# The first projection of a streaming encoder: program order on every engine, two token blocks in turn, a wide norm

## The chip, the cores and the metric

The kernel runs on one core of a Trainium2 chip. The metric is the time of one execution on the device in microseconds. Five engines of the core work side by side, each through its own queue: TensorE (PE, with its weight loads as PEld), VectorE (DVE), ScalarE (ACT), GpSimd (POOL) and SyncE (SP), which here only issues transfers. SBUF holds the working tiles and PSUM the sums of matmuls.

## The reference, cut to what matters

One layer of an encoder, for a prompt of 2048 tokens and a sample of 32, both with D = 1024 channels. The part that the change touches is the beginning:

```python
shift_m, scale_m, gate_m, shift_f, scale_f, gate_f = adaln_modulation(c, p['w_ada'], p['b_ada'])
h = rmsnorm(x, p['g_pre_mix']) * (1.0 + scale_m) + shift_m
z = h @ p['w_in']
qa, ka, va, qb, kb, vb, gb, gk_low, gate_a, gate_b = jnp.split(z, np.cumsum(IN_SIZES)[:-1].tolist(), axis=-1)
```

`adaln_modulation` is `silu(c) @ w_ada + b_ada`, split in six; `rmsnorm` divides a token by the root of its mean square and multiplies with a gain. Attention over a band of chunks, gated linear attention, two gated branches, an output projection and a feed-forward part with a short convolution follow; the change leaves them alone. The columns `qb` and `kb` of `w_in` (256 each) are the first that the kernel computes.

## The kernel before, in words

All tokens (2080, the sample last) stand with channels on the partitions: D is eight pieces of 128, named k. Every product is made in three passes, with operands split in a high part and a rest (`mm3`, lines 78 to 80: high by high, high by rest, rest by high). `hA[0]` and `hA[1]` keep the high part and the rest of `h` for the first 1664 tokens, `hB` for the last 416; `hB` takes the memory of the pool `ada`, once that is closed.

The first projection computes `h` and its products with 512 columns (two chunks of 128 for `Q`, two for `K`) for five blocks b of 416 tokens. The norm goes by half blocks of 208 (`NH`), numbered 0 to 9 (`hb` before, `u` after), since 2048 is inside the last one: there `parts` returns two pieces, 176 tokens of the prompt and 32 of the sample, with scale and shift of their own.

Steps of a half block before the change: `prep_load` (line 262) brings two tiles `xk` of four k each; six buffers. `prep_stats` squares two k at a time on ACT (lines 271 and 274) and adds them (275, 276), on DVE for half blocks 0 and 1, on GpSimd for the others. `rstd_bcast` splits the sum (`sh`, `sl`, lines 69 and 72), sums over partitions with a matmul by ones (148, 149), which also spreads the result, and finishes with Ln, Exp (154, 155) and one Newton step in three DVE operations (156 to 158); the part from the matmul on runs when the function that it returns is called. `prep_apply` then does, for each k, `x * scale * r` on DVE (294), the high part with the shift on ACT (295), and the rest on DVE (296). For half block 2, four k have the first step on GpSimd (`prep_scale`, and line 292).

The scale and shift come from `ada(j, v)`: v = 1 scale, v = 0 shift, j one of four pieces of 256 channels. `ada_load` brings two halves of 512 KB (`wa`, six buffers); 16 matmuls (line 315), a copy to SBUF (318), four matmuls that turn the result (322), and `mod_finish` on DVE (134, 138) into `mod`. So a k can only be shifted after the ada piece of its channels.

`wave(b, ks_, ps, chunks)` runs the matmuls of a block for some k, 12 per k with four chunks. `wave_evac` writes the sums out through `t_evac`: Q chunks are copied on ACT (line 225), K chunks on DVE (228), both to a tile `tx` that has two buffers, and stored to DRAM by a transfer that ACT issues (line 230). The weights of the two column groups come in four pieces each (`w_pieces`, lines 185 to 187: load to `wr`, high part on ACT, rest on DVE).

The order of TensorE's instructions is that of the program text throughout (a `manual_schedule` over PE). The other engines are ordered by the planner of the compiler by priority and its own costs, apart from later stages, which put all five engines in program order. Block 0's waves are laced with the ada pieces by hand; blocks 1 to 4 follow in a loop `s_`, where the half block two ahead is prepared. Behind the first projection, line 515 onwards, come six groups of columns with tokens on the partitions (`n_tile`, matmuls `pn`), beside which bias tables and the late modulation are made.

Of the kernel before, what the change touches and what calls it, by code (L numbers as in the profile page):

```python
# [10 lines left out]
F32 = mybir.dt.float32  # L11
# [9 lines left out]
KD = 8  # L21
# [37 lines left out]
def encoder_step(ctx: ExitStack, tc: tile.TileContext, I, O):  # L59
# [178 lines left out]
    with ExitStack() as st:  # L238
# [16 lines left out]
        XK = {}  # L255
        POOL = {2: (1, 3, 5, 7)}

        def prep_load(hb, q_=nc.sync):
            XK[hb] = []
            for k in range(0, KD, 4):  # L260
                x = pp.tile([128, 4, NH], F32, name="xk", tag="xk", bufs=6)
                q_.dma_start(x, dap(I["xT"], k * 128 * T + NH * hb, [[T, 128], [128 * T, 4], [1, NH]]))
                XK[hb].append(x)

        def prep_stats(hb, add):

            sq = pp.tile([128, 2, NH], F32, name="sq", tag="sq", bufs=2)
            for k in range(0, KD, 2):
                x = XK[hb][k // 4][:, k % 4:k % 4 + 2]
                if k == 0:  # L270
                    nc.scalar.activation(sq, x, AF.Square)
                    continue
                s2 = pp.tile([128, 2, NH], F32, name="sq2", tag="sq2")
                nc.scalar.activation(s2, x, AF.Square)
                add.tensor_add(sq, sq, s2)
            add.tensor_add(sq[:, 0], sq[:, 0], sq[:, 1])
            return lambda: rstd_bcast(pp, psx, "px", sq[:, 0], NH, NH, 2)

        def prep_scale(hb):
            for k in POOL.get(hb, ()):  # L280
                for a, e, s in parts(NH * hb, NH):
                    xs = XK[hb][k // 4][:, k % 4, a:e]
                    nc.gpsimd.tensor_scalar(xs, xs, mod[:, 1, k, s:s + 1], 1.0, op0=OP.mult, op1=OP.mult)

        def prep_apply(hb, r, ks_=range(KD)):
            for k in ks_:
                for a, e, s in parts(NH * hb, NH):
                    hi, lo = [h_at(x, k, NH * hb + a, e - a) for x in range(2)]
                    xs = XK[hb][k // 4][:, k % 4, a:e]
                    s1, s2 = mod[:, 1, k, s:s + 1], mod[:, 0, k, s:s + 1]  # L290
                    if k in POOL.get(hb, ()):
                        nc.gpsimd.tensor_mul(xs, xs, r[:, a:e])
                    else:
                        nc.vector.scalar_tensor_tensor(xs, xs, s1, r[:, a:e], op0=OP.mult, op1=OP.mult)
                    nc.scalar.activation(hi, xs, AF.Identity, bias=s2)
                    nc.vector.scalar_tensor_tensor(lo, xs, s2, f32(hi), op0=OP.add, op1=OP.subtract)
# [3 lines left out]
        def ada_load(j, v):  # L300

            PIECE[j, v] = []
            for half in range(2):
                w = pa.tile([128, 4, 256], F32, name="wa", tag="wa", bufs=6)
                nc.sync.dma_start(w, dap(I["w_ada"], half * 512 * 6 * D + v * D + 256 * j,
                                         [[6 * D, 128], [128 * 6 * D, 4], [1, 256]]))
                PIECE[j, v].append(w)

        def ada(j, v):


            p = psx.tile([128, 512], F32, name="pm", tag="px")
# [5 lines left out]
            nc.vector.tensor_copy(r, p[:, :256])  # L318
# [9 lines left out]
        ln_exp_table()  # L328
        ada_load(0, 1)
        prep_load(0)  # L330
        prep_load(1)
        ada_load(0, 0)
        first = [("Q", 1536), ("K", 1792)]
        w0, steps = zip(*[w_pieces(wp, c0, 256, 272, 2, 2) for _, c0 in first])

        def wave(b, ks_, ps, chunks=range(4)):
            for k in ks_:
                for i in chunks:
                    mm3(ps[i][:, :NB], [t_terms(w0[i // 2], 128 * (i % 2), b, k)], first=k == 0, last=k == KD - 1)

        def wave_tiles():
            return [psx.tile([128, 512], F32, name="px", tag="px") for _ in range(4)]

        def wave_evac(b, ps):
            for i in range(4):
                t_evac(stg, first[i // 2][0], i % 2, b, ps[i][:, :NB])

        fin0 = prep_stats(0, nc.vector)()
        ada_load(1, 1)
        for s_ in steps:  # L350
            s_[0]()
        ada_load(1, 0)
        m0 = ada(0, 1)
        r0 = fin0()
        fin1 = prep_stats(1, nc.vector)()
        m1 = ada(0, 0)
        m0()
        r1 = fin1()
        ps = wave_tiles()
        fins = {}  # L360
        for s_ in steps:
            s_[1]()
        ada_load(2, 1)
        prep_load(2)
        m0 = ada(1, 1)
        m1()
        m1 = ada(1, 0)
        m0()
        ada_load(2, 0)
        ada_load(3, 1)  # L370
        prep_load(3)
        prep_apply(0, r0, [0, 1])
        prep_apply(1, r1, [0, 1])
        for s_ in steps:
            s_[2]()
        ada_load(3, 0)
        fins[2] = prep_stats(2, nc.gpsimd)
        wave(0, (0, ), ps)
        m1()
        m0 = ada(2, 1)  # L380
        prep_apply(0, r0, [2, 3])
        prep_apply(1, r1, [2, 3])
        prep_load(4)
        for s_ in steps:
            s_[3]()
        wave(0, (1, ), ps)
        m0()
        m1 = ada(2, 0)
        fins[3] = prep_stats(3, nc.gpsimd)
        wave(0, (2, ), ps)  # L390
        m1()
        m0 = ada(3, 1)
        prep_apply(0, r0, [4, 5])
        prep_apply(1, r1, [4, 5])
        wave(0, (3, ), ps)
        m0()
        prep_scale(2)
        m1 = ada(3, 0)
        r2 = fins.pop(2)()()
        wave(0, (4, ), ps)  # L400
        m1()
        prep_apply(0, r0, [6, 7])
        prep_apply(1, r1, [6, 7])
        prep_apply(2, r2)
        prep_load(5)
        wave(0, (5, ), ps)
        f3 = fins.pop(3)()
        wave(0, (6, ), ps)
        r3 = f3()
        wave(0, (7, ), ps)  # L410
        prep_apply(3, r3)
        fins[4] = prep_stats(4, nc.gpsimd)
        wave_evac(0, ps)
# [3 lines left out]
        for s_ in range(2, 10):  # L417
            b = s_ // 2
            if s_ + 4 < 10:
                prep_load(s_ + 4)  # L420
            if s_ + 3 < 10:
                fins[s_ + 3] = prep_stats(s_ + 3, nc.gpsimd)
            k0 = 4 * (s_ % 2)
            if s_ + 2 < 10:
                fin = fins.pop(s_ + 2)()
            if s_ % 2 == 0:
                ps = wave_tiles()
            if b < 4:
                wave(b, range(k0, k0 + 1), ps)
                prep_apply(s_ + 2, fin())  # L430
                wave(b, range(k0 + 1, k0 + 4), ps)
            elif s_ % 2 == 0:

                wave(b, range(KD), ps, (0, 1))
                wn = load_w(wp, 2048, 256, 272, 2, 2)
            else:
                wave(b, range(KD), ps, (2, 3))
# [1893 lines left out]
```

## Time and profile before

| | |
|---|---|
| runs shown | 3172.7, 3176.35, 3173.73 us; median 3173.73 |
| the profiled execution, its own time | 3174.99 us |
| its span in the trace | 3173.3 us |
| granted TensorE clock, mean | 0.992 |
| PE, DVE, ACT, POOL busy | 3056.5, 2243.6, 1649.5, 263.7 us |
| first wave of the first projection | starts at 26.86 us |
| last wave of the first projection | ends at 159.66 us |

Times in the trace count from the start of the span. A row of a group of instructions gives line, engine, operation, tile written and tiles read, shapes, count, then busy time and the mean of one in ns, then the idle time ahead of them on that engine with what ended it. A row of the timeline begins with start and length. In a row of waits stand who waited, for whom, the total, how often, and the longest. Queues of transfers are marked with a q behind the engine that issues them.

### The profile page before, as it was taken

What the parts mean: (1) busy time and instruction counts of PE and PEld (TensorE: products, weight loads), DVE (VectorE), ACT (ScalarE), POOL (GpSimd) and SP (SyncE); (2) the same over time, 40 slices, a digit from 0 to 9 for tenths busy, and PEclk for the clock granted to TensorE, in tenths of its full rate; (3) what the DMA queues carried; (4) which work ended last, traced back from release to release, by engine and by line L of the source; (5) the groups of instructions that cost most, each with busy time, mean ns of one, the idle gap of its engine ahead of it and who ended that gap; (6) DMA issues with size and microseconds to landing.
All of it is one profiled execution on the core that took longest, in us unless ns stands there. A gap on an engine that the chain in (4) does not pass through costs nothing. (4 is left out here: it accounts for less than half of the span.)

```text
span 3173.3 us, 56451 instructions
## 1 busy us (share of the span) xinstructions
PE 3056.5 (96%) x19748; PEld 2942.5 (93%) x19748; DVE 2243.6 (71%) x4903; ACT 1649.5 (52%) x3792; POOL 263.7 (8%) x417
## 2 busy tenths in 40 slices
PE   6999999999999999999999999999999999999997
PEld 4899999998999999988999899999999999999997
DVE  6735617774555545566577799998888778897877
ACT  4412224443554545544454655567656556576755
POOL 3201201111111111111000000000000000000001
PEclk9999999999999999999999999999999999999998
DMA  7344435554433333576457686787887667888784
GB/s 226 101 141 127 143 98 143 132 134 132 119 103 110 99 105 117 164 224 194 129 176 223 211 260 208 224 258 227 248 262 218 189 189 231 263 252 280 239 266 148
DMA packets 598799, 580.13 MB, mean 183 GB/s; under 512 B 53201, under 2 KB 527010, under 8 KB 598514
## 3 DMA queue, kind: packets, MB, share of 16 engines
q1 hardware_dynamic: 553826, 528.92, 55.6%
q10 hardware_dynamic: 44432, 47.34, 4.6%
q8 instruction: 155, 2.54, 0.3%
q14 instruction: 130, 1.06, 0.1%
q0 software_dynamic: 256, 0.26, 0.0%
HBM read 388.71 MB, written 187.65 MB: 182 GB/s over the span
## 5 line engine op out<-in xcount | busy, mean ns | idle before, releaser
L1876 PE MATMUL ad<-hA,hB 128*128 128x350 f32 (+2 forms) x1734 | 300.8, 323 | 5.3 <-DVE hB L1818 2.7
L78 PE MATMUL pm<-hA,wh 128*128 128x416 f32 x768 | 290.3, 378 | 0.0
L1876 PEld LDWEIGHTS ad<-hA,hB 128*128 128x128 f32 x1734 | 281.7, 189 | 7.3 <-ACT work L2002 3.8
L79 PE MATMUL pm<-hA,wh 128*128 128x416 f32 x768 | 269.9, 351 | 0.0
L80 PE MATMUL pm<-hA,wl 128*128 128x416 f32 x768 | 269.9, 351 | 0.0
L1818 DVE TENSOR_TENSOR hA<-raws,hA 128x512 fp32r<-128x512 f32 (+1 forms) x367 | 242.0, 668 | 12.5 <-ACT hA L1813 12.2
L1813 ACT ACTIVATE hA<-raws 128x512 fp32r<-128x512 f32 (+1 forms) x367 | 222.0, 617 | 31.7 <-DMA raws<-in_w_up_dram 10.8
L1876 PE MATMUL ad<-hA,hA 128*128 128x348 f32 (+2 forms) x1308 | 226.9, 324 | 3.0 <-ACT work L2002 2.2
L1876 PE MATMUL g<-hA,hB 128*128 128x348 f32 (+2 forms) x1248 | 217.2, 323 | 6.7 <-ACT work L1998 3.9
L1876 PEld LDWEIGHTS ad<-hA,hA 128*128 128x128 f32 x1308 | 213.1, 190 | 4.3 <-ACT work L2002 2.8
L1876 PEld LDWEIGHTS g<-hA,hB 128*128 128x128 f32 x1248 | 202.4, 188 | 9.4 <-ACT work L1998 5.0
L1876 PE MATMUL ad<-hA 128*128 128x350 f32 (+2 forms) x1173 | 204.9, 324 | 4.2 <-DVE hA L1728 4.1
L1876 PEld LDWEIGHTS ad<-hA 128*128 128x128 f32 x1173 | 191.5, 190 | 5.0 <-DVE hA L1728 4.4
L1818 DVE TENSOR_TENSOR hB<-raws,hB 128x512 fp32r<-128x512 f32 (+1 forms) x289 | 191.0, 668 | 6.7 <-ACT hB L1813 6.3
L1813 ACT ACTIVATE hB<-raws 128x512 fp32r<-128x512 f32 (+1 forms) x289 | 175.9, 617 | 26.5 <-DMA raws<-in_w_up_dram 11.6
L69 ACT ACTIVATE pth<-pp 128x256 fp32r<-128x256 f32 (+1 forms) x288 | 106.0, 374 | 145.1 <-PE pp L1023 137.8
L78 PE MATMUL pn<-wh,hA 128*128 128x256 f32 (+1 forms) x624 | 177.8, 285 | 0.0
L79 PE MATMUL pn<-wl,hA 128*128 128x256 f32 (+1 forms) x624 | 177.1, 284 | 0.0
L80 PE MATMUL pn<-wh,hA 128*128 128x256 f32 (+1 forms) x624 | 177.0, 284 | 0.0
L1985 ACT COPY g<-ad 128x348 f32<-128x348 f32 (+2 forms) x102 | 44.3, 434 | 243.1 <-PE ad L1876 155.9
L72 DVE TENSOR_TENSOR ptl<-pp,pth 128x256 fp32r<-128x256 f32 (+1 forms) x288 | 117.5, 413 | 63.6 <-ACT pth L69 61.0
L1876 PE MATMUL g<-hA,hA 128*128 128x350 f32 (+2 forms) x894 | 156.1, 323 | 3.3 <-ACT g L1985 1.7
(505 smaller groups left out, 8470.0 us busy)
## 6 DMA issues: line engine op xcount, KB each, us to landing
raws<-in_w_up_dram SPq DMA_DIRECT2D x220, 256.0 KB, 4.3
raws<-sW SPq DMA_DIRECT2D x176, 256.0 KB, 3.7
sW<-raws SPq DMA_DIRECT2D x88, 256.0 KB, 3.5
raws<-in_w_down_dram SPq DMA_DIRECT2D x80, 256.0 KB, 4.8
wr<-in_w_in_dram SPq DMA_DIRECT2D x76, 256.0 KB, 3.2
sgT<-tx ACTq DMA_DIRECT2D x80, 208.0 KB, 2.7
wa<-in_w_ada_dram SPq DMA_DIRECT2D x64, 256.0 KB, 3.0
keys<-ks SPq DMA_DIRECT2D x128, 128.0 KB, 2.8
```

Source lines behind the costliest of these rows:

```text
L69: i = nc.scalar.activation(hi, src, AF.Copy)
L72: nc.vector.tensor_sub(lo, src, f32(hi))
L78: nc.tensor.matmul(out, ah, bh, start=first and i == 0, stop=False)
L79: nc.tensor.matmul(out, ah, bl, start=False, stop=False)
L80: nc.tensor.matmul(out, al, bh, start=False, stop=last and i == n - 1)
L1813: act = nc.scalar.activation(hi[:, :n], raw(i, n), AF.Copy)
L1818: nc.vector.tensor_sub(lo[:, :n], raw(i, n), f32(hi[:, :n]))
L1876: nc.tensor.matmul(out[:, :w], l_[:, k], r_[:, k, :w], start=first and k == 0 and i == 0, stop=k == n - 1 and i == 2, skip_group_check=True)
L1985: nc.scalar.copy(g[:, 0, :w], ad[:, 0, :w])
```

## The change

The whole first projection goes under a `manual_schedule` of all five engines (`early`), closed at its end. The four loads of half blocks 0 and 1 are issued ahead of the first ada pieces; half block 0 takes two tiles of the pool `ada` (tag `x0`), and `wa` goes from six buffers to five. Nothing runs on GpSimd. The squares of half blocks 0 and 1 have their fourth pair on DVE. The norm is now `mul` (x by r, two or four k in one DVE operation), `shifted` (scale and shift in one ACT operation per k, in place), `high` (one ACT copy for two or four k) and `low` (one DVE subtraction for two or four k). Row sums and ada products use the pool `psm` of two banks. The copy behind an ada product moves from DVE to ACT. Two groups of small matmuls on ones (`idle`) are put ahead of the first wave. The weights come by pairs of k for both column groups (`w_load`, `w_split`). While the ada pieces land, k pairs of block 0 (four chunks) and block 1 (chunks 0 and 1) run in turn; then 40 slots S follow, eight k for: block 1 chunks 2 and 3, block 2, block 3, block 4 chunks 0 and 1, block 4 chunks 2 and 3. The norm of blocks 2 to 4 is dealt out to slots by hand (`at_` from -7 to 2, counted from the slot where the block begins).

```diff
+        early.enter_context(tc.manual_schedule(engines={... ("PE", "Activation", "DVE", "Pool", "SP")}))
+        def x_load(u):
+            pl, tag, n = (pa, "x0", 2) if u == 0 else (pp, "xk", 6)
...
+        def square(u, eng=None):
+            for i in range(4):
+                d = pp.tile([128, 2, NH], F32, name="sq", tag="sq2" if i else "sq", bufs=2 if i else 1)
+                if eng and i == 3:
+                    nc.vector.tensor_mul(d, x_at(u, 2 * i, 2), x_at(u, 2 * i, 2))
+                else:
+                    nc.scalar.activation(d, x_at(u, 2 * i, 2), AF.Square)
+                if i:
+                    nc.vector.tensor_add(SQ[u], SQ[u], d)
+                else:
+                    SQ[u] = d
+            nc.vector.tensor_add(SQ[u][:, 0], SQ[u][:, 0], SQ[u][:, 1])
+        def share(u):
+            return rstd_bcast(pp, psm, "pm", SQ.pop(u)[:, 0], NH, NH, 2)
+        def mul(u, k, n):
+            nc.vector.tensor_mul(x, x, RS[u].unsqueeze(1).to_broadcast([128, n, NH]))
+        def shifted(u, k, n):
+            for y in range(k, k + n):
+                for a, e, s in parts(NH * u, NH):
+                    nc.scalar.activation(x, x, AF.Identity, bias=mod[:, 0, y, s:s + 1], scale=mod[:, 1, y, s:s + 1])
+        def high(u, k, n):
+            nc.scalar.activation(h_of(0, u, k, n), x_at(u, k, n), AF.Copy)
+        def low(u, k, n):
+            nc.vector.tensor_sub(h_of(1, u, k, n), x_at(u, k, n), f32(h_of(0, u, k, n)))
...
-            nc.vector.tensor_copy(r, p[:, :256])
+            nc.scalar.copy(r, p[:, :256])
...
+        def both(b, k):
+            us_ = (2 * b, 2 * b + 1)
+            for u in us_:
+                shifted(u, k, 2)
+                high(u, k, 2)
+            for u in us_:
+                low(u, k, 2)
...
+        x_load(0); x_load(1); ln_exp_table(); ada_load(0, 1); ada_load(0, 0); w_load(0); x_load(2); x_load(3)
+        square(0, "dve"); f0 = share(0); square(1, "dve"); m1 = ada(0, 1); RS[0] = f0(); f1 = share(1)
+        ada_load(1, 1); m0 = ada(0, 0); m1(); RS[1] = f1(); ada_load(1, 0)
+        muls(0, 0); w_split(0); w_load(1); ada_load(2, 1); idle(12); m0(); both(0, 0); idle(16)
+        p0 = wave_tiles(); wave(0, (0, 1), p0)
+        for k in (2, 4, 6):
+            muls(0, k)
+        square(2); RS[2] = share(2)(); square(3); RS[3] = share(3)()
+        muls(1, 0); both(1, 0); p1 = wave_tiles(2)
+        for j in range(1, 4):
+            m1 = ada(j, 1)
+            m0 = ada(j, 0)
+            if j < 3:
+                ada_load(j + 1, 0)
+            m1()
+            m0()
+            w_split(j)
+            if j < 3:
+                w_load(j + 1)
+            if j < 2:
+                ada_load(j + 2, 1)
+            both(0, 2 * j)
+            wave(1, (2 * j - 2, 2 * j - 1), p1, (0, 1))
+            wave(0, (2 * j, 2 * j + 1), p0)
+            muls(1, 2 * j)
+            both(1, 2 * j)
+        x_load(4); x_load(5); wave_evac(0, p0)
...
+        wave(1, (6, 7), p1, (0, 1))
...
+        for S in range(40):
+            B, z = divmod(S, 8)
+            b = B + 1 if B < 4 else 4
+            for c in range(2, 5):
+                U, u0, u1 = 8 * (c - 1), 2 * c, 2 * c + 1
+                at_ = S - U
+                # -7: square(u0)   -6: share(u0)   -5: RS[u0]; square(u1)
+                # -4: mul(u0, 0, 4); shifted(u0, 0, 4); share(u1); mul(u0, 4, 4)
+                # -3: high(u0, 0, 4); RS[u1]; mul(u1, 0, 4); low(u0, 0, 4)
+                # -2: shifted(u1, 0, 4); high(u1, 0, 4); mul(u1, 4, 4)
+                # -1: low(u1, 0, 4); shifted(u0, 4, 4); high(u0, 4, 4)
+                #  0: low(u0, 4, 4); shifted(u1, 4, 4)
+                #  1: high(u1, 4, 4); x_load of the next block   2: low(u1, 4, 4); x_load
+            if S == 0:
+                wave_evac(1, p1, (0, 1))
+            elif z == 0 and B < 4:
+                wave_evac(b - 1, ps, (2, 3) if B == 1 else range(4))
+                ps = wave_tiles()
+            if B == 4 and z == 0:
+                wave_evac(4, ps, (0, 1))
+                wn, pieces = w_pieces(wp, 2048, 256, 272, 2, 2)
+            if B == 4 and z % 2 == 0:
+                pieces[z // 2]()
+            wave(b, (z,), ps, {0: (2, 3), 3: (0, 1), 4: (2, 3)}.get(B, range(4)))
+        wave_evac(4, ps, (2, 3))
+        early.close()
```

In this extract calls that stand on lines of their own are joined by semicolons, and the branches of the slot loop are given as comments. The removed text is the old `prep_` functions, the hand-laced block 0 and the loop `s_`, which the printed functions show.

247 lines of the change are left out of this document (113 added, 134 removed).

## The prediction

> **What bounds the kernel now.** I read the page's busy shares first, then the busy time of each engine by stage (stages cut where the first projection passes from one token block to the next), then the waits inside the first projection.
>
> ```profile
> PE 3056.5 (96%) x19748; PEld 2942.5 (93%) x19748; DVE 2243.6 (71%) x4903; ACT 1649.5 (52%) x3792; POOL 263.7 (8%) x417
> ```
> ```profile
> 0.00:26.86 26.86, 12.54 (x80) 5.98 (x80) 13.09 (x40) 11.67 (x24) 0.70 (x6) 1.00 0.85 262
> 26.86:72.30 45.44, 35.02 (x197) 28.50 (x197) 34.50 (x79) 23.37 (x55) 18.89 (x21) 0.92 0.69 212
> 72.30:99.85 27.55, 20.76 (x97) 18.89 (x98) 22.08 (x48) 15.14 (x37) 13.26 (x12) 0.93 0.32 94
> 99.85:124.83 24.98, 21.08 (x101) 19.52 (x101) 18.83 (x43) 13.33 (x32) 8.66 (x10) 0.94 0.33 96
> 124.83:141.97 17.14, 17.08 (x91) 16.70 (x92) 13.85 (x45) 8.40 (x23) 0.00 (x0) 1.00 0.14 38
> 141.97:159.66 17.69, 17.69 (x96) 17.56 (x95) 13.21 (x37) 6.07 (x15) 0.00 (x0) 1.00 0.64 208
> 160.00:260.00 100.00, 97.25 (x785) 94.46 (x784) 38.56 (x64) 19.52 (x44) 0.00 (x0) 0.98 0.44 138
> ```
>
> The columns are the length, then busy time of PE, PEld, DVE, ACT and POOL, the granted clock, the DMA share and GB/s. TensorE carries the whole kernel and is nearly full after 160 us, so what the first projection gains or loses passes to the end almost one for one. The projection starts at 26.86 and ends at 159.66: 132.8 us. A block without waits takes 17.7 us (last row of the stage), so five take 88.5; some 44 us go to waits, to the ada products and to a slow clock, nearly all before 124.83. That is all the change can win.
>
> ```profile
> POOL sq L275 <- ACT sq L274: 40.0, 20, 5.8
> ACT sq L274 <- POOL sq L275: 11.4, 11, 1.4
> PEld px L78 <- ACT hA L295: 5.9, 5, 2.4
> PEld px L79 <- DVE hA L296: 5.6, 4, 2.0
> DVE tx L228 <- DMA qbT<-tx: 3.6, 2, 2.1
> ```
>
> These waits say that TensorE waits for the norm (lines 295 and 296), and that an evacuation waits for a store to give its buffer back (line 228).
>
> **Prices.** Groups of instructions of the first 160 us, then of the whole run for the wide shapes:
>
> ```profile
> L294 DVE SCALAR_TENSOR_TENSOR xk<-xk,mod,rstd 128x208 f32<-128x208 f32 x68 | 36.2, 575 | 0.4
> L295 ACT ACTIVATE hA<-xk,mod 128x208 fp32r<-128x208 f32 x64 | 26.1, 459 | 20.6 <-DVE xk L294 12.5 <-DVE mod L134 8.0 <-POOL xk L292 0.2
> L274 ACT ACTIVATE sq<-xk 128x416 f32<-128x416 f32 x30 | 16.3, 544 | 17.7 <-POOL sq L275 11.4 <-DMA xk<-in_xT_dram 4.6 <-DVE sq L275 1.7
> L315 PE MATMUL pm<-wa,scp 128*32 128x256 f32 x128 | 12.6, 510 | 7.3 <-DMA wa<-in_w_ada_dram 7.2
> L187 DVE TENSOR_TENSOR wl<-wr,wh 128x512 fp32r<-128x512 f32 x12 | 9.0, 761 | 4.7 <-ACT wh L186 4.5
> L186 ACT ACTIVATE wh<-wr 128x512 fp32r<-128x512 f32 x12 | 7.4, 623 | 9.0 <-DMA wr<-in_w_in_dram 8.9
> L225 ACT ACTIVATE tx<-px 128x416 f32<-128x416 f32 x10 | 4.9, 501 | 5.2 <-PE px L80 5.2
> L228 DVE COPY tx<-px 128x416 f32<-128x416 f32 x8 | 4.7, 584 | 6.0 <-DMA qbT<-tx 3.6 <-ACT rst L154 1.7 <-DMA wa<-in_w_ada_dram 0.6
> L154 ACT ACTIVATE rst<-pst,eps 128x208 f32<-128x208 f32 x10 | 4.2, 425 | 3.8 <-PE pst L149 3.8
> L155 ACT ACTIVATE rst<-rst 128x208 f32<-128x208 f32 x10 | 3.7, 372 | 0.2
> L156 DVE SCALAR_TENSOR_TENSOR rstt<-pst,rst 128x208 f32<-128x208 f32 x10 | 3.7, 370 | 9.6 <-ACT rst L155 9.6
> L69 ACT ACTIVATE sh<-sq 128x208 fp32r<-128x208 f32 x10 | 3.7, 368 | 7.0 <-DVE rstd L158 2.5 <-DVE mod L134 2.5 <-POOL sq L276 1.9
> L275 DVE TENSOR_TENSOR sq<-sq,sq 128x416 f32<-128x416 f32 x6 | 3.6, 592 | 4.2 <-ACT sq L274 4.2
> ```
> ```profile
> L1728 DVE TENSOR_TENSOR hA<-ht,hA 128x696 fp32r<-128x696 f32 x76 | 66.6, 877 | 11.9 <-ACT hA L1727 11.6
> L1727 ACT ACTIVATE hA<-ht 128x696 fp32r<-128x696 f32 x76 | 59.4, 785 | 10.8 <-DMA ht<-aT 5.0 <-DMA ht<-actD 2.6 <-DMA ht<-hT 1.6
> L1891 ACT ACTIVATE work<-ad,cw 128x696 f32<-128x696 f32 x44 | 41.2, 937 | 2.2 <-DVE ad L1886 1.8 <-DVE ad L2013 0.4
> ```
>
> From 416 to 696 elements a DVE tensor_tensor grows from 592 to 877 ns and an ACT copy from 501 to 785, 1.0 ns an element; so one of 832 (four k at once) is about 1.0 us on DVE and 0.9 on ACT. Timeline rows for starts, spacing and clock:
>
> ```profile
> 7.55 1.08 PE L315 MATMUL pm<-wa,scp 128*32 128x256 f32 x8 [0.32 <-DMA wa<-in_w_ada_dram]
> 16.21 1.94 PE L315 MATMUL pm<-wa,scp 128*32 128x256 f32 x16
> 16.89 0.38 PEld L315 LDWEIGHTS pm<-wa,scp 128*32 128x32 f32 x8 [0.48 <-DMA wa<-in_w_ada_dram]
> 18.07 1.02 PE L322 MATMUL pm<-sel,mr 128*128 128x2 f32 x4
> 20.36 0.54 PE L148 MATMUL pst<-sh,ones 128*128 128x208 f32 x1 [1.27 <-ACT sh L69]
> 25.11 1.54 ACT L295 ACTIVATE hA<-xk,mod 128x208 fp32r<-128x208 f32 x4 [1.89 <-DVE mod L134]
> 60.34 0.55 PE L78 MATMUL px<-hA,wh 128*128 128x416 f32 x1
> 60.68 0.55 PE L79 MATMUL px<-hA,wh 128*128 128x416 f32 x1
> 124.80 0.33 ACTq L230 DMA_DIRECT2D qbT<-tx  x1
> 127.77 0.59 DVE L228 COPY tx<-px 128x416 f32<-128x416 f32 x1 [2.10 <-DMA qbT<-tx]
> DMA to landing us min/median/max: 1.9/2.0/4.1
> ```
>
> Four ACT operations of 208 in 1.54 us are 0.38 each. Matmuls come 0.34 us apart after an idle stretch, against 0.184 in the last block. A store holds its `tx` buffer 1.9 to 4.1 us (last row, stores of `tx`); I take 2.4.
>
> **The change part by part.**
>
> *Order of loads.* SP issues four token loads (1.70 MB), then `ada_load(0, 1)`, `ada_load(0, 0)` (1.05 MB each). In the profile the same 3.8 MB have landed at 16.89, when the last half of (0, 0) comes; so (0, 0) is there at the same time, but (0, 1), alone first before (7.55), now comes at about 13.3 (1.7 MB more, at the pace of the two rows: 2.75 MB in 9.34 us). Squares of blocks 0 and 1 (0.54 each) end by 14 and are covered. Then a chain in order: ada(0, 1) to 14.4 (1.08); row-sum matmuls 0.9 (two of 0.54, overlapping), Ln and Exp 0.8, first DVE step 0.4, to 16.5, which frees the second `pm` bank; ada(0, 0) at 16.89, 1.94 to 18.9; transposes 1.02 and the addition of the bias; second row sum 0.9 to 21.1; Ln, Exp, three steps to 23.1; two multiplies 1.1; two weight subtractions 1.4 to 25.6; the shift; on ACT four shifts and two copies 2.6; the last subtraction 0.6 to 28.9. The first wave starts near 28.9 instead of 26.86. `idle(12)` and `idle(16)`, 28 matmuls of 128 columns, lie in TensorE's waits for the multiplies and for `high`, and cost nothing; without that cover they would cost 28 times 0.11 (0.34 cut from 416 columns to 128), some 3 us.
>
> *The first wave pair and the second block's norm.* 24 matmuls, half of them slow: to 35.3. Now program order bites: `square(2)`, `share(2)()`, `square(3)`, `share(3)()` run one after the other on ACT and DVE behind six multiplies, and both row sums stand on TensorE ahead of ada(1, 1). Row sum 2 falls at 35.5, Ln to the last step ends at 38, the adds of block 3 follow, row sum 3 is at 41: TensorE idles 5 us. Two ada products at 1.94 end at 45.8; ACT copies them only after `both(1, 0)` at 47; transposes, weight split, shifts and `both(0, 2)` to 52.7, with 12 matmuls at 0.34 beside it; 24 matmuls to 58.3.
>
> *Rounds j = 2 and 3.* Per round TensorE has two ada products (1.0 each at full clock), transposes 1.1, 12 matmuls 2.2, 24 matmuls 4.4; it waits some 0.5 for ACT's copies and 1.4 for the last `low`: 11.4, twice, to T = 81.1. There block 0 is done, and 12 matmuls are left of the half of block 1 taken along. In the old kernel block 0 ends at 72.3; TensorE has done 36 matmuls more here. After T there are 336 matmuls, 61.9 us at 0.184. With no wait the stage would end at 143, 16.6 us before the old 159.66.
>
> *Evacuation.* `tx` has two buffers. Q0, Q1 fill both on ACT; K0, K1 on DVE wait for their stores (2.4); the stores of K0, K1 are issued by ACT, so ACT stands until 4.1 us after Q0 began, 3.1 more than its own work of two copies. Queued behind it: the next squares or `high`. After T two such turns follow each other (block 0, then the two chunks of block 1), so `square(4)` starts at T + 6 (its tokens, asked for when `low(1, 6, 2)` gives their buffer back near T - 5, are there). [...]
>
> *Norm of one block, blocks 2 to 4.* Counted from ACT's first square, u0 and u1 the halves: two squares 1.0, add 0.6 (frees a `sq2` buffer), fourth square 0.55, add 0.6, half add 0.37 (as line 156, the same 208 elements), `sh` and `sl` 0.75, row sum 0.4, Ln and Exp 0.8, three steps 1.2: 6.4. Adds of u1 behind them: 8.6. `mul` 1.0, four shifts 1.6: 11.2. `sh`, `sl`, row sum 1.1; Ln to last step 2.1; `mul` 1.0; shifts 1.6; `high` 0.9; `low` 1.0: k 0 to 3 ready at 18.9. The other half keeps ACT until 22.5, with the evacuation of the block before inside it 26.6 (23.2 at block 2, whose turn holds only K), `low` 1 later. That is longer than 17.7, and each row sum stands on TensorE ahead of a wave. GpSimd's 41.5 us (sum of the POOL column) go; since these prices are those of operations without it (0.38 to 0.43 against line 294's mean of 575 ns), no more comes off.
>
> *The sum.* T + 6: squares of block 2; its wave at T + 24.9, where TensorE with no wait would be at T + 11. Block 3's squares T + 29.2, wave T + 48.1; block 4's squares T + 55.8, its first half T + 75.9, its second half (sixteen shifts more for the two-sequence part, 2.4, and the evacuation, 4.1) T + 85.8. From there 4.4 + 8.85 us of matmuls and 1.5 of slow clock: T + 100.8 = 181.9. Minus 159.7: +22.2. The split of the next weight lies inside the last 8.85 us. The profiled execution took 3174.99 (span 3173.3, 1.7 around it), which gives 3197.2; it lies 1.3 above the median of 3173.73, on which I forecast 3196.
>
> Bounds. A shift with two pointers is not in the first stage: at least line 295's 0.38, at most 0.155 more (line 1891 against 1727); I take the low end since its shape is the nearer; the other adds up to 9. A gap's restart: nothing to 13 matmuls at 0.16, 2 us, two or three on the path. Stores 1.9 or 4.1: -2 to +7. The planner orders what follows anew: about 5 either way, an estimate from the 2.75 us that the stage loses at 160 to 260.
>
> **The rivals.**
> *Faster: the norm keeps up.* For it: in 124.83 to 159.66 TensorE never waits, and per block ACT needs about 16 us and DVE 16, less than 17.7. [...] The time: end at 143, 3157. Against it: the squares of block 2 stand behind two evacuations and behind nothing else that could go first, and the block's chain of 18.9 us has 8.85 us of matmuls beside it. It decides if `square(4)` starts before T - 7.
> *No change.* The waits after T are half of my 39 us, so that they eat the 16.6 us won: 3174. For it: overlap of neighbouring operations (0.09 each) that I dropped in places.
> *Slower still.* Shifts at the high end and cold restarts: +13, 3209.
>
> **How the numbers follow.** Forecast 0.56, norm keeps up 0.15, no change 0.09, slower still 0.20. Within 0.2% (6.3 us, about what a measurement here tells from nothing) lies only the third: faster 0.15, same 0.09, slower 0.76. The range goes from 3172 to 3214 and leaves out the fast rival and the tails; the forecast's own is 3184 to 3206.
>
> **What would show it.** First wave at 28 to 30; block 0's last matmul near 81; row sums of halves 4 to 9 each with a TensorE wait of 2 to 5 us before it; ACT idle 2 to 4 us at each K store; block 2 near 106; stage end near 182; POOL idle. Wrong it would be if the squares of block 2 start before block 0 ends, or if ACT passes a waiting store.

## The result and the profile after

| | before | after |
|---|---|---|
| median of the runs | 3175.04 us (4 runs) | 3213.54 us (4 runs) |
| the profiled execution, its own time | 3174.99 us | 3214.19 us |
| its span | 3173.3 us | 3211.8 us |
| last wave of the first projection ends | 159.66 us | 197.86 us |
| first matmul behind the projection | 160.12 us | 198.06 us |

The changed kernel is slower: ratio 1.0116, 95% interval 1.0098 to 1.0135, some 38.5 us. The fourth run of the kernel before, 3182.78 us, is not among the three shown earlier; with it the median is 3175.04 instead of 3173.73. Slower is the predicted direction. The time lies inside the range (3172 to 3214), but 0.5 us under its end, 17.5 us above the forecast of 3196, outside the forecast's own 3184 to 3206, and nearer to the rival "slower still" (3209). Of the 39.2 us between the two profiled executions, 37.9 have come up by the first matmul behind the projection, so the stage holds the loss. The busy line of the changed kernel's page:

```profile
PE 3075.0 (96%) x19776; PEld 2958.8 (92%) x19776; DVE 2227.3 (69%) x4813; ACT 1677.8 (52%) x3826; POOL 224.2 (7%) x377
```

Nothing in it tells of the loss: busy shares hardly moved, and no engine but TensorE is over 69%. Cut into stretches, with the columns of the first table of stages, it shows. The cuts are the first wave, a point just behind the end of block 0 (some 83.4), a point just behind the first matmul of block 2's wave, a point ahead of the copies of block 2, the first wave of block 4 and the end of the stage:

```profile
27.87:84.30 56.43, 44.64 (x261) 37.41 (x262) 28.19 (x60) 33.22 (x70) 0.00 (x0) 0.91 0.44 138
84.30:113.80 29.50, 16.03 (x61) 13.94 (x60) 14.14 (x24) 13.67 (x29) 0.00 (x0) 0.77 0.23 73
113.80:140.00 26.20, 21.35 (x94) 19.97 (x95) 15.92 (x27) 17.12 (x35) 0.00 (x0) 0.87 0.29 82
140.00:170.00 30.00, 22.87 (x107) 20.58 (x106) 15.23 (x26) 18.02 (x39) 0.00 (x0) 0.94 0.22 63
170.00:197.86 27.86, 21.55 (x95) 20.12 (x96) 13.10 (x25) 10.68 (x22) 0.00 (x0) 0.82 0.41 134
200.00:300.00 100.00, 97.18 (x785) 94.22 (x785) 36.28 (x61) 19.10 (x44) 0.00 (x0) 0.98 0.45 134
```

In the second row TensorE, DVE and ACT are each busy about half of 29.5 us: nobody is full, which fits engines that work one after the other. Behind the stage (last row) TensorE's 97.18 us in 100 equals the 97.25 of before, so nothing is given back. The waits inside the stage, a selection (who waited for whom, total, times, longest):

```profile
PE pst L148 <- ACT sh L69: 24.8, 7, 8.1
ACT xk L293 <- DVE xk L287: 19.1, 10, 2.5
DVE hA L302 <- ACT hA L299: 18.6, 19, 1.7
DVE tx L228 <- DMA qbT<-tx: 14.7, 6, 4.3
ACT tx L225 <- DMA kbT<-tx: 8.0, 2, 7.0
```

TensorE waits for the row sums (line 148); ACT waits for DVE's multiplies and DVE for ACT's copies, in turn; both wait for stores that hold `tx`. The turn at the end of block 0, on ACT and then on DVE:

```profile
82.43 0.50 ACT L225 ACTIVATE tx<-px 128x416 f32<-128x416 f32 x1
82.97 0.35 ACTq L230 DMA_DIRECT2D qbT<-tx  x1
83.92 0.33 ACTq L230 DMA_DIRECT2D qbT<-tx  x1
87.69 3.03 ACTq L230 DMA_DIRECT2D kbT<-tx  x2
90.89 0.52 ACT L225 ACTIVATE tx<-px 128x416 f32<-128x416 f32 x1 [7.00 <-DMA kbT<-tx]
93.34 1.43 ACT L275 ACTIVATE sq<-xk 128x416 f32<-128x416 f32 x3 [0.40 <-ACT tx L225]
...
118.80 1.42 ACT L275 ACTIVATE sq<-xk 128x416 f32<-128x416 f32 x3
149.00 1.41 ACT L275 ACTIVATE sq<-xk 128x416 f32<-128x416 f32 x3
```
```profile
87.06 0.59 DVE L228 COPY tx<-px 128x416 f32<-128x416 f32 x1 [3.91 <-DMA qbT<-tx]
89.77 0.59 DVE L228 COPY tx<-px 128x416 f32<-128x416 f32 x1 [2.11 <-DMA qbT<-tx]
```

DVE's copy of the first K chunk waits until 87.06 for the store issued at 82.97; ACT cannot issue that chunk's store until 87.69, and its own next copy, of block 1's Q, needs the buffer that this store gives back. So ACT does nothing for 7.00 us. Only at 93.34 come the first squares of block 2. The squares of blocks 3 and 4 follow at 118.80 and 149.00. TensorE meanwhile:

```profile
27.87 0.72 PE L78 MATMUL px<-hA,wh 128*128 128x416 f32 x1 [0.79 <-ACT hA L299]
40.74 0.39 PE L148 MATMUL pst<-sh,ones 128*128 128x208 f32 x1 [4.88 <-ACT sh L69]
97.22 0.54 PE L148 MATMUL pst<-sh,ones 128*128 128x208 f32 x1 [8.05 <-ACT sh L69]
112.84 0.45 PE L78 MATMUL px<-hA,wh 128*128 128x416 f32 x1 [1.51 <-ACT hA L299]
```

### The profile page after: what moved, and what is told of

Its sections match the earlier page's. It is cut to its first block, busy times and chain, and to the rows that moved or that the text cites. A ratio compares the mean times of both kernels' runs of the same rounds, so it can differ in the third digit from the quotient of the medians.

```text
span 3211.8 us, 56446 instructions
## 1 busy us (share of the span) xinstructions
PE 3075.0 (96%) x19776; PEld 2958.8 (92%) x19776; DVE 2227.3 (69%) x4813; ACT 1677.8 (52%) x3826; POOL 224.2 (7%) x377
## 5 line engine op out<-in xcount | busy, mean ns | idle before, releaser
L1870 ACT ACTIVATE hA<-raws 128x512 fp32r<-128x512 f32 (+1 forms) x367 | 221.9, 617 | 30.5 <-DMA raws<-in_w_up_dram 10.7
L1870 ACT ACTIVATE hB<-raws 128x512 fp32r<-128x512 f32 (+1 forms) x289 | 175.9, 617 | 26.6 <-DMA raws<-in_w_up_dram 12.5
```

Of the source, the lines that this page charges most:

```text
L1870: act = nc.scalar.activation(hi[:, :n], raw(i, n), AF.Copy)
```

## The experiments

The time differences below are each taken against the kernel before as it ran in the same group (3177.7 to 3179.1 us); "stage end" is the start of the first matmul behind the projection, 160.12 before and 198.06 after.

| kernel | median us | ratio to before, 95% | us to before | stage end |
|---|---|---|---|---|
| e1 after, only TensorE in program order | 3185.78 | 1.0024 [1.0013, 1.0035] | +8.1 | 170.75 |
| e2 after, four `tx` | 3208.16 | 1.0095 [1.0080, 1.0110] | +30.5 | 190.73 |
| e3 after, no sums for half blocks 4 to 9 | 3177.10 | 1.0001 [0.9991, 1.0010] | -0.6 | 156.45 |
| e4 before, norm without GpSimd | 3170.94 | 0.9975 [0.9965, 0.9985] | -6.7 | 153.18 |
| e5 e4, norm in wide operations | 3180.96 | 1.0007 [0.9997, 1.0016] | +1.9 | 161.58 |
| e6 e4, half of it wide | 3175.76 | 0.9995 [0.9985, 1.0004] | -3.3 | 156.85 |
| e7 after, K stores issued by SP | 3215.96 | 1.0120 [1.0102, 1.0138] | +36.9 | 200.10 |
| e8 after, waves ahead of the norm | 3215.16 | 1.0109 [1.0089, 1.0129] | +36.1 | 197.87 |
| e9 e4, row sums in `pm` banks | 3165.99 | 0.9957 [0.9945, 0.9970] | -12.9 | 149.89 |
| e10 e9, four `tx` | 3170.37 | 0.9973 [0.9964, 0.9982] | -8.5 | 149.39 |
| e11 before, tokens ahead of ada weights | 3177.14 | 0.9995 [0.9986, 1.0004] | -1.8 | 160.87 |
| e12 after, first squares ahead of the copies | 3210.21 | 1.0103 [1.0086, 1.0120] | +31.3 | 192.04 |

**The order of ACT, DVE and SP (e1).** One statement goes; TensorE stays in program order, the planner orders the rest.

```diff
-        early.enter_context(tc.manual_schedule(engines={... ("PE", "Activation", "DVE", "Pool", "SP")}))
```

> The changed kernel with one thing undone: only TensorE stays in program order in the first projection, the other four engines go back to the planner; all operations, tiles and loads stay those of the changed kernel. Theory (ACT and DVE in program order make one chain per block longer than the block's matmuls, and hold squares behind evacuations): squares of block 2 start well before block 0 is evacuated, the stage ends at 172 to 183 instead of 197.7, total 3188 to 3200. Rival (the wide norm with two-pointer shifts is itself what costs): order gives nothing, 3210 to 3216. Rival (row sums on TensorE ahead of waves, which keep their place here): also about 3210.

3185.78, a little under the expected band: 30 of the 38.5 us go (8.1 left), and the stage ends 27.3 us earlier. The timeline of ACT in this run shows squares of block 2 between two copies, and the stretch 84 to 114, to be read against 84.30:113.80 above, is fuller on all three engines:

```profile
78.97 0.52 ACT L225 ACTIVATE tx<-px 128x416 f32<-128x416 f32 x1
79.38 0.54 ACT L273 ACTIVATE sq<-xk 128x416 f32<-128x416 f32 x1
...
87.00 0.52 ACT L225 ACTIVATE tx<-px 128x416 f32<-128x416 f32 x1 [3.78 <-DMA kbT<-tx]
```
```profile
84.00:114.00 30.00, 20.62 (x85) 18.86 (x85) 16.88 (x29) 18.45 (x38) 0.00 (x0) 0.77 0.32 100
```

ACT does 18.45 us of work there instead of 13.67. The number of instructions on each engine is the same over the whole run; what differs is the order in which each queue holds them.

**The norm's sums as the chain (e3).** Squares, sums and row sums of half blocks 4 to 9 left out.

```diff
-                if at_ == -7:
-                    square(u0)
-                elif at_ == -6:
-                    fins[u0] = share(u0)
-                elif at_ == -5:
-                    RS[u0] = fins.pop(u0)()
-                    square(u1)
+                if at_ == -5:
+                    RS[u0] = RS[3]
+                    RS[u1] = RS[3]
...
-                    fins[u1] = share(u1)
...
-                    RS[u1] = fins.pop(u1)()
```

> The changed kernel without squares, sums and row sums of half blocks 4 to 9; they use the factors of half block 3 (so these blocks' norm is left out of the computation). Theory (the chain of a block, 22 to 30 us, is the bound of blocks 2 to 4, and statistics are some 10 us of it): the chain falls under the 17.7 us of a block's matmuls, TensorE waits only once after block 1, stage end 158 to 166, total 3174 to 3182. Rival (clock at half speed after idle stretches, or shifts with two pointers, are the cost): at most 10 us come off, 3203 to 3213.

The time is as expected, and the stage ends at 156.45, 41.6 us earlier and 1.5 before the expected band, although ACT's busy time in the whole run falls by 19.4 us (1677.8 to 1658.4) and DVE's by 22.3 (2227.3 to 2205.0). Taking away the first half of the chain is worth about the sum of both, as it would be if the two engines work in turns; the granted clock rises too, from 0.77 to 0.94 in the stretch, where TensorE's busy time per matmul falls from 0.26 to 0.20 us; what share of the gain that is no run separates. The stretch of the second row above, in this run:

```profile
84.30:113.80 29.50, 25.66 (x128) 24.80 (x127) 15.81 (x18) 20.06 (x37) 0.00 (x0) 0.94 0.49 142
```

**Waves ahead of the norm on TensorE (e8).**

```diff
+            if z:
+                wave(b, (z,), ps, {0: (2, 3), 3: (0, 1), 4: (2, 3)}.get(B, range(4)))
...
-            wave(b, (z,), ps, {0: (2, 3), 3: (0, 1), 4: (2, 3)}.get(B, range(4)))
+            if z == 0:
+                wave(b, (z,), ps, {0: (2, 3), 3: (0, 1), 4: (2, 3)}.get(B, range(4)))
```

(the first two lines stand at the head of each slot)

> The changed kernel with the wave of a slot placed ahead of the slot's norm on TensorE (except in the first slot of each eight), so that the row sums stand behind one more wave; order on ACT and DVE is the same. Theory (ACT's and DVE's chain is the bound, the row sums only show it): stage end 195 to 199, total 3209 to 3216. Rival (row sums ahead of waves are the loss): 9 us or more come off, below 3204.

No change, stage end 197.87. So the largest wait of the list, TensorE on the row sum, is where the lateness shows and not what makes it: with a wave put ahead of it the stage ends at the same time within 0.2 us.

**Stores that hold `tx` (e2, e7).** Four buffers (three small tiles of the ada products use the `nx` buffers, for the room), or K stores issued by SP:

```diff
-        x = stg.tile([128, NB], F32, name="tx", tag="tx")
+        x = stg.tile([128, NB], F32, name="tx", tag="tx", bufs=4 if kind in "QK" else None)
```
```diff
-        nc.scalar.dma_start(dst[128 * c:128 * c + 128, cols], x)
+        (nc.sync if kind == "K" else nc.scalar).dma_start(dst[128 * c:128 * c + 128, cols], x)
```

> The changed kernel with four tx buffers instead of two for the Q and K chunks (room made by keeping scp, mr and ns in tiles that are idle then). Theory (evacuation turns hold ACT, and behind ACT the squares): square of block 2 near 86 instead of 93.3, the two later turns 3 us shorter each, stage end near 185, total 3198 to 3203. Rival (stores do not hold ACT, or the chain hides them): 3211 to 3216.

> The changed kernel with the stores of K chunks issued by SP instead of ACT. Theory (ACT is held by a store ahead of it in its queue): the turns at blocks 2 and 3 give back 3 us each (ACT goes on with high and squares), the first turn little, since block 1's Q chunks still wait for the buffers; stage end 190 to 193, total 3206 to 3210. Rival (DVE, held by the same wait, keeps the squares back anyway): 3211 to 3216.

Four buffers brought 8 us of time and 7.3 of stage, about half of what I expected. The squares start at 89.69 instead of 93.34, since the wait moved by one turn: with four buffers the copies of block 1's Q wait for those same stores.

```profile
83.42 1.17 ACTq L230 DMA_DIRECT2D kbT<-tx  x2
87.30 0.52 ACT L225 ACTIVATE tx<-px 128x416 f32<-128x416 f32 x1 [4.33 <-DMA qbT<-tx]
89.69 1.43 ACT L275 ACTIVATE sq<-xk 128x416 f32<-128x416 f32 x3 [0.40 <-ACT tx L225]
```

With the stores on SP nothing was won in the end, a miss. The expected step did come: in the turn of block 2, `high`, whose shifts ended near 143.4 in both kernels, no longer waits behind the two K stores (first the changed kernel, then e7):

```profile
148.19 0.90 ACT L299 ACTIVATE hA<-xk 128x832 fp32r<-128x832 f32 x1 [3.14 <-DVE tx L228]
145.07 0.90 ACT L299 ACTIVATE hA<-xk 128x832 fp32r<-128x832 f32 x1 [0.40 <-ACT tx L225]
```

The squares of block 2 came at 90.02 instead of 93.34 for another reason. There ACT's next copy needs the buffer of the K chunk in any case; but DVE's two K copies started at 84.05 and 86.44 instead of 87.06 and 89.77, since the Q stores issued at 82.02 and 82.97 gave their buffers back after 2.0 and 3.5 us instead of 4.1 and 5.85:

```profile
84.05 0.59 DVE L228 COPY tx<-px 128x416 f32<-128x416 f32 x1 [1.84 <-DMA qbT<-tx]
86.44 0.59 DVE L228 COPY tx<-px 128x416 f32<-128x416 f32 x1 [1.79 <-DMA qbT<-tx]
```

The two Q stores stand 0.95 us apart in both kernels. What differs is SP: in the changed kernel it sends three token loads of 416 KB between 78.93 and 83.55, right beside the stores; in e7 the last two of them (for block 3) stand behind the K stores. The row of the changed kernel:

```profile
78.93 4.62 SPq L264 DMA_DIRECT2D xk<-in_xT_dram  x3
```

What was won so was lost again, because now SP stood:

```profile
84.67 29.95 SPq L230 DMA_DIRECT2D kbT<-tx  x4
114.71 2.13 SPq L264 DMA_DIRECT2D xk<-in_xT_dram  x4
```
```profile
118.52 0.99 ACT L275 ACTIVATE sq<-xk 128x416 f32<-128x416 f32 x2 [3.57 <-DMA xk<-in_xT_dram]
```

Four issues took 29.95 us of SP's sequence, from 84.67 on, most of it a wait for block 1's K chunks, and the token loads behind them went out at 114.71, where the changed kernel had sent the last two at 81.69 and 83.18. So ACT waited 3.57 us for the tokens of block 3 (6.16 for those of block 4). A store that waited for its data held the queue it stood in, SP's here (four issues in 29.95 us) as ACT's before (`high` at 148.19 instead of 145.07).

**First squares ahead of the copies (e12).** One statement moved, to test the step that the prediction leaned on most.

```diff
         x_load(5)
+        square(4)
         wave_evac(0, p0)
...
                 if at_ == -7:
-                    square(u0)
+                    if c > 2:
+                        square(u0)
```

> The changed kernel with one statement moved: square(4) stands ahead of the evacuation of block 0 instead of behind both evacuations. Theory (block 2's squares behind the evacuation start the chain late, and the time after that is one chain of ACT and DVE steps): squares at 82.5 to 84.5 instead of 93.3; the two copies of Q come 2 us later, so the evacuation ends about 2 us later and the next ACT step of the norm waits for it; block 2's wave 2 to 4 us earlier than 112.8, stage end 194 to 196, 3209 to 3212. Rival A (the whole 10.9 us of the hold is lost to the place of the squares): wave near 102, stage end near 187, 3203. Rival B (evacuation holds the projection's banks, and block 1's second pair comes later by as much): no change, 3214 or a little more.

Squares at 81.98 instead of 93.34, but block 2's wave at 108.89 instead of 112.84: 11.4 us earlier at the head, 3.95 at the wave. The evacuation, still ahead of `sh`, kept the rest.

```profile
81.98 1.42 ACT L275 ACTIVATE sq<-xk 128x416 f32<-128x416 f32 x3
88.89 0.86 ACTq L230 DMA_DIRECT2D kbT<-tx  x2
90.93 0.52 ACT L225 ACTIVATE tx<-px 128x416 f32<-128x416 f32 x1 [5.41 <-DMA kbT<-tx]
92.85 0.38 ACT L69 ACTIVATE sh<-sq 128x208 fp32r<-128x208 f32 x1 [0.40 <-ACT tx L225]
108.89 0.45 PE L78 MATMUL px<-hA,wh 128*128 128x416 f32 x1 [1.54 <-ACT hA L299]
```

The theory's wave held, and its time (3209 to 3212); the stage ended 2 us earlier than it said (192.04 against 194 to 196). These 2 us come piece by piece: 4.3 us earlier at the copies of block 2's Q (143.27 to 138.96), 4.8 where the last 72 matmuls begin (180.85 to 176.06), 6.0 at the end. The last 1.2 go with the clock: the mean granted clock over these matmuls is 0.80 in the changed kernel and 0.87 in e12 (they come 0.35 us or more apart for 6.8 us in the changed kernel, until 187.62, and for 4.0 us in e12, until 180.06, and 0.19 after that). What makes the rest I did not follow further.

**The parts done alone on the kernel before.** Loads (e11):

```diff
-        ada_load(0, 1)
...
+        ada_load(0, 1)
```

(moved behind the loads of half blocks 0 and 1)

> The kernel before with one edit: the tokens of block 0 and 1 are asked for ahead of the ada weights of half (0, 1). Theory (the loads' order is a side issue: 3.8 MB must land before the first wave either way): first wave at 27 to 28 (26.9 before), time within 3 us of the kernel before, ratio 0.999 to 1.001. Rival (the loads' order is a good part of the 9 us that the changed kernel loses with a planned order): 5 us or more slower, ratio above 1.0015.

No difference that can be measured; the first wave starts at 25.37 instead of 26.86, before even the expected 27 to 28, and the stage ends 0.75 later. The tokens ahead of the weights neither gain nor cost anything by themselves.

GpSimd out of the norm (e4), the wide form of it on top (e5), the wide form for the first four k alone (e6):

```diff
-        POOL = {2: (1, 3, 5, 7)}
+        POOL = {}
...
-        fins[2] = prep_stats(2, nc.gpsimd)
+        fins[2] = prep_stats(2, nc.vector)
```

(the same for half blocks 3 to 9)

```diff
+        def wide(hb, r, k, n):
+            x = XK[hb][k // 4][:, k % 4:k % 4 + n]
+            nc.vector.tensor_mul(x, x, r.unsqueeze(1).to_broadcast([128, n, NH]))
+            for y in range(k, k + n):
+                for a, e, s in parts(NH * hb, NH):
+                    xs = XK[hb][y // 4][:, y % 4, a:e]
+                    nc.scalar.activation(xs, xs, AF.Identity, bias=mod[:, 0, y, s:s + 1], scale=mod[:, 1, y, s:s + 1])
+            hi, lo = [h_at(z, slice(k, k + n), NH * hb, NH) for z in range(2)]
+            nc.scalar.activation(hi, x, AF.Copy)
+            nc.vector.tensor_sub(lo, x, f32(hi))
```

> The kernel before, with GpSimd's part of the norm given to DVE (adds of squares of half blocks 2 to 9, and the plain form for half block 2); nothing else changed. Theory: dropping GpSimd alone is not what lost the time; DVE takes about 17 us more work over 100 us, but no longer runs its first step at 575 ns: 3168 to 3182. Rival (dropping GpSimd overloads DVE and is the loss): 3190 or more.

> The kernel before without GpSimd (the last run's fourth kernel, stage end 152.8, 3170.9 us), with the changed kernel's form of the norm everywhere: one wide multiply, a two-pointer shift per k in place, one wide copy, one wide subtraction; order, loads and rounds stay the old ones under the planner. Theory (the form is no loss, order is): DVE work of a block falls from about 20 to 15 us, ACT's rises from 14 to 18; stage end 148 to 158, total 3166 to 3177. Rival (the wide form itself is a good part of the loss: three ACT steps in a row, and ACT at 18 us a block above the 17.7 of the matmuls): stage end 162 or later, 3180 or more.

> As the run before, but the wide form only for k 0 to 3 of half blocks 2 to 9; k 4 to 7 and the first two half blocks keep the narrow form. DVE about 17.5 us a block, ACT about 16, both under 17.7. Theory: the best of the three, stage end 144 to 151, 3162 to 3169. Rival (ACT's longer chain before the first k): no gain, 3170 to 3178.

Without GpSimd the old kernel is faster: -6.7 us, stage end 153.18. Two views of the norm's first DVE step (least, median and longest duration in ns, over all shapes), of the kernel before and of e4, show one reason:

```profile
L294 DVE SCALAR_TENSOR_TENSOR xk<-xk,mod,rstd x84: 244/425/1341, 20.1 to 144.9; 128x208 f32<-128x208 f32 x68, 128x176 f32<-128x176 f32 x8, 128x32 f32<-128x32 f32 x8
```
```profile
L294 DVE SCALAR_TENSOR_TENSOR xk<-xk,mod,rstd x88: 242/427/436, 19.6 to 138.0; 128x208 f32<-128x208 f32 x72, 128x176 f32<-128x176 f32 x8, 128x32 f32<-128x32 f32 x8
```

The median is the same; with GpSimd's adds running, single steps took up to 1341 ns, without them none took over 436. The longest began at 117.12, beside a GpSimd add (line 275) from 117.15 to 118.23; what makes such steps long no run here shows. ACT's step (line 295) shows no such effect: its mean is 459 ns in both. There is a second reason that no run here separates from the first: GpSimd's adds of squares are slower than DVE's, so without them the chain of sums is shorter too (the kernel before, then e4):

```profile
L275 POOL TENSOR_TENSOR sq<-sq,sq 128x416 f32<-128x416 f32 x24 | 29.6, 1231 | 40.2 <-ACT sq L274 40.0
L275 DVE TENSOR_TENSOR sq<-sq,sq 128x416 f32<-128x416 f32 x30 | 17.6, 588 | 9.3 <-ACT sq L274 8.4 <-ACT sq L271 0.9
```

The wide form takes the gain back, and both expectations for it (3166 to 3177, and 3162 to 3169 on half of the k) missed on the slow side. Per k it is four operations over two engines, DVE, ACT, ACT, DVE, where the old form has three, DVE, ACT, DVE. On ACT the new `shifted`, with two pointers, is no cheaper than the old step that also wrote the high part (549 ns against 459), and the high part comes on top:

```profile
L291 ACT ACTIVATE xk<-xk,mod 128x208 f32<-128x208 f32 x72 | 34.9, 549 | 12.2 <-DVE mod L134 9.7 <-DVE xk L287 2.5
L293 ACT ACTIVATE hA<-xk 128x832 fp32r<-128x832 f32 x12 | 10.6, 886 | 0.1
L294 DVE TENSOR_TENSOR hA<-xk,hA 128x832 fp32r<-128x832 f32 x12 | 12.3, 1025 | 15.2 <-ACT hA L293 15.2
```
```profile
L295 ACT ACTIVATE hA<-xk,mod 128x208 fp32r<-128x208 f32 x64 | 25.7, 459 | 18.5 <-DVE xk L294 10.0 <-DVE mod L134 8.2
L296 DVE SCALAR_TENSOR_TENSOR hA<-xk,mod,hA 128x208 fp32r<-128x208 f32 x64 | 24.4, 427 | 1.0 <-ACT hA L295 1.0
```

(the first three of e5, the last two of e4). A subtraction that covers four k waits for all four shifts and the copy: DVE's idle time before it is 15.2 us, against 1.0 with one k at a time. Over the whole run DVE's busy time falls by 16.8 us (2242.3 to 2225.5) and ACT's grows by 23.5 (1648.7 to 1672.2). TensorE's waits for `high`, of e5 and then of e4:

```profile
PE px L78 <- ACT hA L293: 9.7, 4, 5.3
```
```profile
PE px L78 <- ACT hA L295: 2.1, 1, 2.1
```

Wide on half of the k (e6) lies between, 3.4 us behind e4.

**A version that beats both (e9, e10).** In e4 TensorE still waited 3.8 us for DVE's copy of `tx`, at the row sum's matmul (line 148), which takes its bank from the projection's six. In e9 row sums use the ada products' two banks.

```diff
-            return lambda: rstd_bcast(pp, psx, "px", sq[:, 0], NH, NH, 2)
+            return lambda: rstd_bcast(pp, psm, "pm", sq[:, 0], NH, NH, 2)
```

> The kernel before with the norm's GpSimd adds on VectorE (as in the run without GpSimd), and the row sums of the norm in the `pm` banks instead of the `px` banks. Theory (row sums queue for a projection bank that an evacuation still holds; that run's wait of the row sum for VectorE's copy of `tx`, 3.8 us, goes): 3165 to 3169 against a kernel before of 3177, ratio 0.996 or lower. Rival (another chain stands right behind, the projection's waits for `hA` and `hB` take the same time): 0.9975 as without this edit, stage end 153.

> The same and four buffers for `tx` (three small tiles of the ada products moved into the `nx` buffers for the room). Theory that stores holding `tx` still cost the planned order something: 2 to 4 us less than with two buffers, stage end 149 to 151. Rival (the planner already lays other work into those waits, 1.7 us a turn at most): within 1 us of the kernel with two buffers.

3165.99: the wait for `tx` is gone from the list, the stage ends 3.3 us earlier than e4's. Four `tx` buffers on top gave nothing: the stage ends 0.5 us earlier, the median is 4.4 us higher, and the intervals overlap. Perhaps the planner already puts other work into the wait, so that more buffers have nothing left to free; that is not shown. e9 is the best kernel measured, 0.43% (0.30 to 0.55%) under the kernel before. Its median is one of five runs, and its interval still touches that of e4 (0.9945 to 0.9970 against 0.9965 to 0.9985).

## Why the prediction was right, point by point

**Direction and mechanism were right, the size was short.** The stage lost 38.2 us by its last wave where 22.2 were forecast, and that the time still fell inside the range is partly luck: two of the four runs, 3214.19 and 3214.64 us, lie above it. Of its signs the first wave (27.87), the idle GpSimd and the row sums that TensorE waits for came, though the waits before the six row sums of blocks 2 to 4 ran from 1.75 to 8.05 us and not from 2 to 5; ACT's idle time at the K stores was 7.00, 0.65, 3.14 and 3.06 us; block 2 came at 112.84 and not near 106, the stage end at 197.86 and not near 182. Two slips of arithmetic stand in the working: after T there are 348 matmuls and not 336 (480 in all, less 96 and 36), so the end without waits and with it the fast rival's time would be some 2 us later; and the last step of the sum adds 14.75 us, not 15.0.

**Up to the end of block 0 it held.** First wave 28.9 predicted, 27.87 measured; row sum of half block 3 at 41 with 5 us of idle TensorE, measured 40.74 with 4.88. A round took about 12.2 us instead of 11.4 (second wave pairs at 66.16 and 78.33), so block 0 ended near 83.4 instead of 81.1: 2.3 us.

**The place of the squares was right, the size of the hold was not.** `square(4)` was forecast at T + 6, 87.1; it came at 93.34, T + 9.9. The term that failed is the store's hold of `tx`, taken at 2.4 us: from the issue of the two Q stores to the K copies it was 4.1 (82.97 to 87.06) and 5.85 (83.92 to 89.77), and from the first K store to the next Q copy 3.2 (87.69 to 90.89). The row of before gave 4.1 as its longest, and that end was the nearer here. That the stores follow each other closely is not the reason: in the turn of block 3 two Q stores 1.0 us apart (175.87 and 176.87) were followed by K copies at 177.87 and 178.91, 2.0 us behind each. The likely reason is the token loads that SP sends beside them, since e7, which holds two of these back, got the buffers after 2.0 and 3.5 us; the prediction had no term for transfers of another queue, and no run holds back the loads alone. That a waiting store holds ACT, which the sum took as given and no row of the prediction shows, is right by the runs, and the later turns show it best: `high` at 148.19, behind the K stores and 3.14 us of idle time, and at 145.07 in e7 without them.

**The chain was right in kind and a little short in its terms.** From the squares to block 2's k 0 to 3 ready 18.9 was predicted, 20.5 measured (93.34 to 113.85); to block 3's squares 23.2 against 25.5; from block 3's to block 4's 26.6 against 30.2; from there to the last `low` 30 against 32.9 (149.00 to 181.85). The shift with two pointers is a term of it that I put at the low bound of 0.38; four take 1.91, 0.48 each:

```profile
103.56 1.91 ACT L293 ACTIVATE xk<-xk,mod 128x208 f32<-128x208 f32 x4 [2.19 <-DVE xk L287]
```

Sixteen shifts a block make 1.6 us more for each of blocks 2 and 3 and some 1.4 for block 4 (9.87 us on ACT, with the two-sequence ones, where 8.5 was counted): 4.6 in all. The stores made 3.9 at block 0 and 1.3 in the two later turns, which took ACT 4.9 and 4.55 us (143.27 to 148.19, 175.35 to 179.90) instead of 4.1 each. On the path the differences add up as 2.3 for the rounds, 3.9 for the hold, 2.3, 3.6 and 2.9 for the chain from one block's squares to the next, and 1.0 behind the last `low`: 16.0, which is 197.86 less the predicted 181.9. Of the chain's share the shifts and the later turns are 5.9; the other 2.9 are spread over its steps (the factor of block 2's first half, for one, was ready 6.95 us behind the squares and not 6.4). The remaining 1.3 us of the difference between the two profiles lies behind the stage, well inside the 5 allowed for it. The rival "slower still" (3209) had the same mechanism and the shifts at their high end; it lacked the stores, which weigh as much.

**The fast rival fell where it was said to.** It needed `square(4)` before T - 7. No run brought the squares so early; e12 brought them to about T - 1.4 and the stage 6 us down; e1, where the planner orders ACT, DVE and SP, brought 27 us. The rival had TensorE never wait after T; it did wait: in the second stretch it was busy 16.03 of 29.50 us, and no other engine was fuller.

**GpSimd was undervalued.** The prediction took the steps' prices without GpSimd beside them, so it had the effect in its sum, but read the removal as nothing more. Measured alone it pays: -6.7 us. So does, by the stage end, the move of the row sums to the `pm` banks, which is also a part of the change: 3.3 us in e9. By stage ends the change is a sum of: GpSimd out, 160.1 to 153.2; the wide form, to 161.6; TensorE's new order, two blocks in turn and the new order of loads with the planner on the other engines, to 170.75; program order on these, to 198.06. The third step is a difference of two kernels that differ in several parts; of these only the loads, which cost nothing, and the row sums' banks, which gained, were tried alone, so what in it costs the 9.2 us stays open.

## What to carry to other kernels

When every engine of a stage is half busy (here TensorE, DVE and ACT 16.03, 14.14 and 13.67 of 29.50 us), count the chain and not the engines: here a step that waited stopped all that stood behind it in its queue, a DMA issue as much as an operation (`high` on ACT came at 148.19 instead of 145.07, the token loads of SP in e7 at 114.71 instead of 81.69), so a written order should put independent work ahead of it. Fewer, wider operations need a reader that does not wait for the whole of them; here the wide form, on the kernel without GpSimd, lowered DVE's busy time by 16.8 us and ended the stage 8.4 us later. A change of several parts is worth taking apart, since one of the parts here, alone, made the kernel faster, and a second one, on top of it, ended the stage earlier.

## What the runs showed of the hardware that was not expected

- With GpSimd's adds running, single DVE steps of line 294 took up to 1341 ns, in e4 without them none over 436; ACT steps of line 295 kept their mean of 459.
- Four DMA issues on SP took 29.95 us in e7, where their data was not ready, and the token loads behind them left from 114.71 on, the first 33.0 us later than in the changed kernel (81.69).
- Two stores of `tx`, 0.95 us apart, held their buffers 4.1 and 5.85 us with token loads of SP in flight beside them, and 2.0 and 3.5 us in e7, where two of these loads left later; in the profile of before the median from issue to landing was 2.0 and the longest 4.1.
